# Moving the stream and one weight tile of the feed-forward products to other start addresses in SBUF

## The chip, the cores and the metric

The kernel runs on one core of one Trainium2 chip. The metric is the device time of one execution in microseconds, median of several runs. "Profiled execution" is one run taken with the hardware profiler; its span goes from the first to the last instruction.

## The reference

One decoder layer on 512 positions of 1024 channels: a gated short convolution and a sparse attention are merged into the residual stream, and then a convolutional feed-forward block follows. The change touches the feed-forward block alone, which is

```python
h = rmsnorm(x, norm2_g[l])
gu = h @ w_ffn_in[l]
g = causal_dwconv(gu[..., :D_FF], ffn_conv_w[l]) + ffn_conv_b[l]
x = x + (jax.nn.silu(g) * gu[..., D_FF:]) @ w_ffn_out[l]
```

with `D_FF` = 2816, that is 22 tiles of 128 channels, for the gate half and for the up half of `w_ffn_in`.

## The kernel before

**Precision.** Every operand of a large product is kept as two float32r tiles, a rounded one (`..h`) and the rest (`..l`). A product is three matmuls for each block of 128 input channels: high weight by high stream, high weight by low stream, low weight by high stream. `dense` (L402) issues the first two for all blocks (L405, L406), and then the third for all blocks (L408). In the profile the instructions carry these three lines, whatever product they belong to, so one goes by tile names.

**The products.** `h @ w_ffn_in` is made in blocks of 2 x 2 with seven products in place of eight (Strassen's scheme in Winograd's form). The stream is the normed input: `xf_h` and `xf_l` (L829, L830) hold for each of 4 blocks of input channels 7 forms of 256 positions, T4, B11 and so on, and they stay in SBUF for the whole stage. The weights come for two channel tiles `f`, `f+1` at a time. `ff_forms` (L898) loads two raw tiles and makes from them the seven weight forms: a22 as `th`/`tl` (two buffers, half the width), a11 and a12 side by side in the ring tiles `wh_s`/`wl_s`, and the four sums in `sh`/`sl`. `ff_pair` (L942) then runs the seven products, each with 4 blocks of input channels, so 12 matmuls of 256 moving columns against 128 x 128 weights, and adds the results on VectorE. Their PSUM banks are called `p1`, `p26`, `p45`, `p37`; the profile leaves numbers out and calls them all `p`. The first product of a pass is a22 by T4 (L977), on `th` and `tl`; then a11 and a12, on `wh_s` and `wl_s`; then the sums, on `sh` and `sl`.

**The order of the stage.** `ff_strassen` (L992) is called for f = 0, 2, ... 20. It makes a pass for the gate half (n = 0) and one for the up half (n = 1), so there are 22 passes of 84 matmuls. Behind each pass `between` runs at most one piece of the down projection by `w_ffn_out` (`down_part`, L1013), whose matmuls have 512 moving columns and write `pdn`. Pieces exist from f = 4 on; the scheduler that orders the instructions put some of the early ones in the middle of a pass. From f = 8 on each pass is followed by two tiles of the down projection, 24 matmuls of `pdn`, and then by the `th` matmuls of the next pass.

**Where things lie.** A tile pool lays its tiles out in SBUF one behind the other, in the order in which their tags first appear, so an unused tile of the right size moves all that follows in its pool. Such tiles are called `gap_..` here. Most tiles are multiples of 512 bytes a partition, and so it is enough to speak of a start as so many bytes behind a multiple of 512. Almost all matmul operands of this kernel begin at 480, the stationary ones and the moving ones, the down projection's included. In the program before, `gap_x` (80 words, 320 bytes) stands ahead of `xf_h` and `xf_l`, which so begin at bytes 37152 and 65824 of each partition, both 288 behind a multiple of 512. The pool `pw` follows. A placeholder named `th_` takes the two `th` buffers first, at 94496 and 96544, also 288 behind. Then `gap_w` (48 words, 192 bytes) brings all later tiles, `tl`, `sh`, `sl` and the rest, back to 480. `wh_s` and `wl_s` lie in another pool, at 480 too. Inside the tiles, the pieces that a matmul reads are 512 or 1024 bytes apart, so they begin at the same distance as their tile.

Of the kernel before, what the change touches and what calls it, by code (L numbers as in the profile page):

```python
# [11 lines left out]
F32 = mybir.dt.float32  # L12
# [6 lines left out]
P = 128  # L19
# [63 lines left out]
def tile_block(ctx: ExitStack, tc: tile.TileContext, xT, pos, par, par2, w_tok, w_a3, w_gate, w_ao, w_bo, w_o,  # L83
# [12 lines left out]
    def const(shape, name, dt=F32, pool=sb):  # L96
        return pool.tile(shape, dt, name=name, tag=name)
# [724 lines left out]
    B11, T4, B21, B22, T1, T3, T2 = range(7)  # L822
    px = ctx.enter_context(tc.tile_pool(name="px", bufs=1, side="left"))
    x1 = pxg.tile([P, KD, S], F32, name="x1", tag="xg_h", bufs=1)
    const([P, 80], "gap_x", F32, px)
    O_ORDER = (0, 4, 1, 5, 2, 6, 3, 7)
    for j in O_ORDER:
        nc.sync.dma_start(x1[:, j], xT[:, j])
    xf_h = const([P, 4, 7, TH], "xf_h", F32R, px)  # L829
    xf_l = const([P, 4, 7, TH], "xf_l", F32R, px)  # L830
    pw = ctx.enter_context(tc.tile_pool(name="pw", bufs=1, side="left"))
    pw.tile([P, D // 2], F32R, name="th_", tag="th", bufs=2)
    const([P, 48], "gap_w", F32, pw)

    def x_forms(k, v):
        nc.vector.tensor_sub(v[:, T1:T3 + 1], v[:, 1:4:2], v[:, 0:2])
# [273 lines left out]
```

## Time and profile before

| | us |
|---|---|
| median of 3 runs | 715.39 |
| lowest and highest | 714.96, 718.07 |
| profiled execution | 715.21 |
| its span | 713.5 |

The page counts 4285 matmuls (PE) and as many weight loads (PEld), 957 instructions on VectorE (DVE), 722 on ScalarE (ACT) and 179 on GpSimd (POOL). The feed-forward products run from about 363 to 682 us of the span. The timeline merges neighbouring equal instructions into a row with a count; a row's first number is the start of its first instruction in us. The length of a single matmul that the profile gives (276 to 284 ns for the feed-forward products) is longer than the distance to the next start, because matmuls are pipelined and their ends are modelled.

### The profile page before, as it was taken

How to read it: one execution, taken by the hardware profiler on the slowest of the kernel's cores; microseconds unless marked ns; L12 is line 12 of the kernel's file. 1: busy time of each engine (PE TensorE's matmuls, PEld its weight loads, DVE VectorE, ACT ScalarE, POOL GpSimd, SP SyncE). 2: the span in 40 equal slices, each digit the busy share in tenths (PEclk: the TensorE clock that was granted, in tenths of full speed). 3: DMA queues.
4: the chain of work that ended last, by engine and by line, in shares of the span. 5: the costliest groups of instructions: out<-in, count | busy, mean ns of one | idle time of the engine just before them, and what ended most of it. 6: DMA issues, size and time to landing. Idle time of an engine off the chain costs nothing.

```text
span 713.5 us, 11375 instructions
## 1 busy us (share of the span) xinstructions
PE 708.3 (99%) x4285; PEld 633.5 (89%) x4285; DVE 534.8 (75%) x957; ACT 432.6 (61%) x722; POOL 182.4 (26%) x179
## 2 busy tenths in 40 slices
PE   9999999999999999999999999999999999999997
PEld 9999878888888888888889999899999999999986
DVE  6887886687566878365795899988787877878643
ACT  7535655977667776522676767666555765647440
POOL 4051422133433334433012220221211222111110
PEclk9999999999999999999999999999999999999999
DMA  7333687511121122336386797987978779785565
GB/s 274 97 95 119 172 181 162 135 60 59 60 69 51 60 76 73 118 128 197 94 197 137 174 236 196 226 209 183 213 183 211 175 185 206 185 198 105 123 142 149
DMA packets 41142, 105.47 MB, mean 148 GB/s; under 512 B 3968, under 2 KB 9216, under 8 KB 41088
## 3 DMA queue, kind: packets, MB, share of 16 engines
q1 hardware_dynamic: 26528, 70.41, 30.4%
q0 software_dynamic: 14272, 34.08, 27.6%
q8 instruction: 33, 0.54, 0.3%
q10 hardware_dynamic: 288, 0.26, 0.1%
q14 instruction: 21, 0.17, 0.1%
HBM read 102.64 MB, written 2.10 MB: 147 GB/s over the span
## 4 chain that ended last, share of the span: by engine, by line
PE 96%; DMA 2%; ACT 1%; issue 0%; DVE 0%; POOL 0%; ACTq 0%; POOLq 0%
PE p L406 9%; PE p L405 9%; PE p L408 9%; PE pdn L406 6%; PE pdn L405 6%; PE pdn L408 6%; PE pg L406 4%; PE pg L405 4%; PE pg L408 4%; PE pa L405 2%; PE pt L681 2%; PE pa L406 2%; PE pa L408 2%; PE po L405 2%; PE po L406 2%; PE po L408 2%
## 5 line engine op out<-in xcount | busy, mean ns | idle before, releaser
L406 PE MATMUL p<-xf_l,sh 128*128 128x256 f32 x336 | 80.6, 277 | 0.0
L405 PE MATMUL p<-xf_h,sh 128*128 128x256 f32 x336 | 80.5, 277 | 0.0
L153 ACT ACTIVATE sh<-s 128x1024 fp32r<-128x1024 f32 x44 | 46.2, 1057 | 38.2 <-PE p L406 24.7
L406 PE MATMUL pdn<-al,wh_d 128*128 128x512 f32 x176 | 68.8, 391 | 0.0
L405 PE MATMUL pdn<-ah,wh_d 128*128 128x512 f32 x176 | 68.5, 390 | 0.0
L405 PEld LDWEIGHTS p<-xf_h,sh 128*128 128x128 f32 x336 | 63.0, 188 | 0.1
L406 PEld LDWEIGHTS p<-xf_l,sh 128*128 128x128 f32 x336 | 63.0, 188 | 0.1
L161 POOL DMA_DIRECT2D wl_s<-in_w_ff_dram x22 | 19.5, 885 | 167.2 <-ACT wl_s L160 155.9
L154 DVE TENSOR_TENSOR sl<-s,sh 128x1024 fp32r<-128x1024 f32 x44 | 53.8, 1224 | 8.7 <-ACT sh L153 8.7
L159 ACT ACTIVATE wh_s<-wr_s 128x1024 fp32r<-128x1024 f32 x22 | 23.3, 1059 | 53.1 <-PE pdn L406 50.1
L408 PE MATMUL p<-xf_h,sl 128*128 128x256 f32 x336 | 51.5, 277 | 0.0
L136 POOL TENSOR_TENSOR wl_g<-wr_g,wh_g 128x1024 fp32r<-128x1024 f32 x16 | 38.4, 2401 | 50.7 <-ACT wh_g L134 25.4
L405 PE MATMUL pg<-xg_h,wh_g 128*128 128x512 f32 x128 | 50.7, 396 | 0.0
L406 PE MATMUL pg<-xg_l,wh_g 128*128 128x512 f32 x128 | 50.6, 395 | 0.0
L408 PE MATMUL pdn<-ah,wl_d 128*128 128x512 f32 x176 | 47.7, 389 | 0.0
L161 POOL DMA_DIRECT2D wl_d<-in_w_dn_dram x22 | 26.5, 1203 | 77.2 <-ACT wl_d L160 69.0
L1029 DVE TENSOR_TENSOR x<-x,pdn 128x512 f32<-128x512 f32 x48 | 33.0, 688 | 16.2 <-PE pdn L408 15.5
L408 PEld LDWEIGHTS p<-xf_h,sl 128*128 128x128 f32 x336 | 44.6, 188 | 0.2
L405 PE MATMUL p<-xf_h,wh_s 128*128 128x256 f32 x168 | 40.5, 276 | 0.0
L406 PE MATMUL p<-xf_l,wh_s 128*128 128x256 f32 x168 | 40.5, 276 | 0.0
L408 PEld LDWEIGHTS pdn<-ah,wl_d 128*128 128x128 f32 x176 | 33.0, 188 | 6.9
L406 PEld LDWEIGHTS pdn<-al,wh_d 128*128 128x128 f32 x176 | 33.0, 188 | 6.2
(359 smaller groups left out, 2123.1 us busy)
## 6 DMA issues: line engine op xcount, KB each, us to landing
wr_s<-in_w_ff_dram SPq DMA_DIRECT2D x44, 512.0 KB, 4.9
wl_s<-in_w_ff_dram POOLq DMA_DIRECT2D x22, 512.0 KB, 7.2
wr_d<-in_w_dn_dram SPq DMA_DIRECT2D x22, 512.0 KB, 7.0
wl_d<-in_w_dn_dram POOLq DMA_DIRECT2D x22, 512.0 KB, 8.2
wr_g<-in_w_gate_dram SPq DMA_DIRECT2D x16, 512.0 KB, 3.4
wr_a<-in_w_a_dram SPq DMA_DIRECT2D x12, 512.0 KB, 4.1
tl<-in_w_ff_dram POOLq DMA_DIRECT2D x22, 256.0 KB, 6.9
wl_a<-in_w_a_dram POOLq DMA_DIRECT2D x10, 512.0 KB, 7.9
```

The source lines that it names most:

```text
L136: e.tensor_sub(lo[:, 0:n], raw[:, 0:n], hi[:, 0:n].bitcast(F32))
L153: hi = nc.scalar.activation(h, v, AF.Copy)
L154: nc.vector.tensor_sub(l, v, h.bitcast(F32))
L159: nc.scalar.activation(h, raw, AF.Copy)
L161: nc.gpsimd.dma_start(l if dst is None else dst, src, accum_op=ALU.add)
L405: nc.tensor.matmul(acc, wh, xh, start=first and i == 0, stop=False)
L406: nc.tensor.matmul(acc, wh, xl, start=False, stop=False)
L408: nc.tensor.matmul(acc, wl, xh, start=False, stop=last and i == len(units) - 1)
L681: nc.tensor.transpose(pt[:, i * P:(i + 1) * P], e[:, i, (kt + k0) * P:(kt + k0 + 1) * P], ident)
L1029: nc.vector.tensor_add(xj, xj, acc)
```

## The change

Two unused tiles change size, and one of them changes place. `gap_x` becomes 112 words, 448 bytes, so `xf_h` and `xf_l` begin at 37280 and 65952, 416 behind a multiple of 512. `gap_w` becomes 16 words, 64 bytes, and stands ahead of `th_`, so the two `th` buffers begin at 94688 and 96736, 480 behind. The two gaps together are 128 words before and after, so no other tile moves. The instructions of every engine and their order are the same in both programs.

```diff
@@ -822,15 +822,15 @@
     px = ctx.enter_context(tc.tile_pool(name="px", bufs=1, side="left"))
     x1 = pxg.tile([P, KD, S], F32, name="x1", tag="xg_h", bufs=1)
-    const([P, 80], "gap_x", F32, px)
+    const([P, 112], "gap_x", F32, px)
     O_ORDER = (0, 4, 1, 5, 2, 6, 3, 7)
...
     pw = ctx.enter_context(tc.tile_pool(name="pw", bufs=1, side="left"))
+    const([P, 16], "gap_w", F32, pw)
     pw.tile([P, D // 2], F32R, name="th_", tag="th", bufs=2)
-    const([P, 48], "gap_w", F32, pw)
```

## The prediction

> **What bounds the kernel now.** I read the page's first two parts and the chain that ended last, then the windows of the feed-forward stage, then the timeline of TensorE row by row.
>
> ```profile
> PE 708.3 (99%) x4285; PEld 633.5 (89%) x4285; DVE 534.8 (75%) x957; ACT 432.6 (61%) x722; POOL 182.4 (26%) x179
> PEclk9999999999999999999999999999999999999999
> PE 96%; DMA 2%; ACT 1%; issue 0%; DVE 0%; POOL 0%; ACTq 0%; POOLq 0%
> ```
>
> TensorE works without a break, at full clock, and is 96% of the chain. So only the pace at which one matmul follows another can move the end; the other engines, the queues and the DMAs do the same work as before and have room. The busy time of a matmul is modelled and says little here. What counts is the distance from one start to the next, which I call the pitch.
>
> The edit moves the two moving tiles of the products `p` (`xf_h`, `xf_l`) and one weight tile (`th`). How many of these matmuls stand where is shown by the windows of the instructions that write `p` (columns: stretch, length, busy time and count of matmuls, clock, DMA):
>
> ```profile
> 359.50:397.50 38.00, 21.02 (x170) 1.00 0.75 163
> 397.50:420.50 23.00, 23.00 (x204) 1.00 0.80 194
> 420.50:437.50 17.00, 15.34 (x130) 1.00 0.89 225
> 437.50:477.50 40.00, 21.51 (x175) 1.00 0.90 214
> 477.50:683.50 206.00, 136.15 (x1176) 1.00 0.78 180
> ```
>
> By the code there are 22 passes (11 values of `f`, times gate and up) of 84 matmuls, 1848 in all, each with 256 moving columns: 12 on `th`/`tl`, and 72 on the other forms. The windows add to 1855 because a matmul across an edge counts twice.
>
> **Three paces of the same matmul.** The timeline of one pass late in the stage (start, length of the merged row, line, operation, count; a row of x4 is four matmuls):
>
> ```profile
> 476.65 1.07 PE L408 MATMUL pdn<-ah,wl_d 128*128 128x512 f32 x4
> 477.55 0.28 PE L405 MATMUL p<-xf_h,th 128*128 128x256 f32 x1
> 477.67 0.28 PE L406 MATMUL p<-xf_l,th 128*128 128x256 f32 x1
> ...
> 478.50 0.62 PE L408 MATMUL p<-xf_h,tl 128*128 128x256 f32 x4
> 478.96 0.28 PE L405 MATMUL p<-xf_h,wh_s 128*128 128x256 f32 x1
> ...
> 487.12 0.39 PE L405 MATMUL pdn<-ah,wh_d 128*128 128x512 f32 x1
> ```
>
> Eight matmuls with `th` take 477.55 to 478.50, 0.95/8 = 118.8 ns each. The 72 that follow take 478.96 to 487.12, 8.16/72 = 113.3 ns. The `pdn` matmuls ahead have 512 columns and take (477.55 - 476.65)/4 = 225 ns, the same per column: this is the stream's own pace, and nothing I found in the feed-forward stage goes below it for long. Call 113.3 the fast pace.
>
> An earlier pass, whose last `th` matmul alone stands behind a down projection:
>
> ```profile
> 462.11 1.07 PE L408 MATMUL pdn<-ah,wl_d 128*128 128x512 f32 x4
> 463.02 0.28 PE L406 MATMUL p<-xf_l,th 128*128 128x256 f32 x1
> 463.14 0.63 PE L408 MATMUL p<-xf_h,tl 128*128 128x256 f32 x4
> 463.61 0.28 PE L405 MATMUL p<-xf_h,wh_s 128*128 128x256 f32 x1
> ...
> 472.09 0.39 PE L405 MATMUL pdn<-ah,wh_d 128*128 128x512 f32 x1
> ```
>
> The same 72 matmuls, on the same tiles at the same addresses, take 463.61 to 472.09: 8.48/72 = 117.8 ns. TensorE waits for nobody in either pass. So there are two stable paces for one and the same pair of addresses (moving at 288 behind a multiple of 512, weights at 480), and a pass stays in the one it fell into for its whole length. What decides is how it was entered. Behind eight `th` matmuls, whose weights also lie at 288, it runs fast. Where a down projection hands over straight to a weight at 480, it runs slow. Two more such hand-overs:
>
> ```profile
> 421.71 0.28 PE L405 MATMUL p<-xf_h,sh 128*128 128x256 f32 x1
> ...
> 426.19 0.40 PE L406 MATMUL p<-xf_l,sh 128*128 128x256 f32 x2
> ...
> 450.65 0.28 PE L406 MATMUL p<-xf_l,sh 128*128 128x256 f32 x1
> 450.77 0.28 PE L405 MATMUL p<-xf_h,sh 128*128 128x256 f32 x1
> 450.88 0.28 PE L406 MATMUL p<-xf_l,sh 128*128 128x256 f32 x1
> 451.00 0.28 PE L408 MATMUL p<-xf_h,sl 128*128 128x256 f32 x1
> 451.12 0.39 PE L405 MATMUL pdn<-ah,wh_d 128*128 128x512 f32 x1
> ```
>
> The four at 450.65 take 0.47 us, 117.5 ns each; the stretch from 421.71 to 426.19, 38 matmuls, (426.19 - 421.71)/38 = 117.9 ns. I found no hand-over from a settled down projection to a weight at 480 that ran fast at once.
>
> When `th` follows a fast pass directly it is slower still, 406.84 to 407.80, 0.96/8 = 120 ns, and yet the 72 behind it run fast (408.26 to 416.42, 8.16 us):
>
> ```profile
> 406.84 0.28 PE L405 MATMUL p<-xf_h,th 128*128 128x256 f32 x1
> ...
> 407.80 0.62 PE L408 MATMUL p<-xf_h,tl 128*128 128x256 f32 x4
> 408.26 0.28 PE L405 MATMUL p<-xf_h,wh_s 128*128 128x256 f32 x1
> ...
> 416.42 0.28 PE L405 MATMUL p<-xf_h,th 128*128 128x256 f32 x1
> ```
>
> So `th` at the address of the moving operand costs 118.8 - 113.3 = 5.5 ns a matmul, and at the same time sets the rest of the pass on the fast pace. My reading, which is an inference: the weight load of the next matmul and the moving stream of this one get in each other's way, by how their addresses and starts stand to each other, and the slow pace is the one in which the weight load is late.
>
> **The change part by part.** No instruction is added, removed or reordered on any engine, and no DMA; only three kinds of address differ.
>
> (a) `th` goes from 288 to 480. What it removes is the price of equal addresses: 22 passes x 8 x 5.5 ns = 0.97 us, if these matmuls then run at the fast pace. What goes with it is the cover: the kick that put 14 of 14 passes behind 477.5 on the fast pace. After the change each such pass is a hand-over from a down projection straight to a weight at 480, the kind that ran slow in each case above.
>
> (b) `xf_h` and `xf_l` go from 288 to 416, so that the weights at 480 begin 64 bytes ahead of the stream instead of 192. The trace has no such pair for a 256-column product. From above it is bounded by the dearest pace seen, 120 ns; from below by the stream's own, 113.3. The nearest rows are the two paces of the pair 288 and 480, since there too stream and weights begin apart; between them I take the slow one, because of (a), and keep both ends. That other distances act alike is suggested by the scores, where 512 columns start at 352 in one place and at 96 in another, both against weights at 480 and both entered from settled projections:
>
> ```profile
> 99.45 0.40 PE L602 MATMUL sc<-kk,qT 128*128 128x512 f32 x1
> 99.69 0.39 PE L603 MATMUL sc<-kk,qT 128*128 128x512 f32 x1
> 99.91 0.40 PE L602 MATMUL sc<-kk,qT 128*128 128x512 f32 x1
> ...
> 127.14 0.40 PE L602 MATMUL sc<-kk,qT 128*128 128x512 f32 x1
> 127.37 0.39 PE L603 MATMUL sc<-kk,qT 128*128 128x512 f32 x1
> 127.59 0.39 PE L405 MATMUL pa<-xg_h,wh_a 128*128 128x512 f32 x1
> ```
>
> The two matmuls take 0.46 us at 352 and 0.45 us at 96: at these two distances the address makes no difference.
>
> **The sum for the likeliest case**, all passes slow. Behind 477.5: 1176 matmuls, 14 x 8 = 112 of them on `th`. 1064 x (117.8 - 113.3) ns = +4.8 us, 112 x (117.8 - 118.8) = -0.1 us. Between 397.5 and 437.5: 334 matmuls less about 38 that are slow already and 32 on `th`: 264 x 4.5 = +1.2 us. Before 397.5 and from 437.5 to 477.5 the passes are slow already: nothing. Together +5.9 us; small differences in how the down projections settle I put at -0.2 us (an estimate). The profiled execution took 715.21 us (713.5 us of span and 1.7 around it), close to the median of 715.39. 715.2 + 5.7 = 720.9 us. The ACT, DVE and POOL work beside it gets 0.3 us more time a pass, so nothing new waits.
>
> **The rivals.**
>
> *All passes fast* (faster side). If 64 bytes apart settles on 113.3 ns from any entry, `th` gains 0.97 us and the slow stretches go: 170 + 175 + 38 matmuls less about 45 on `th`, 338 x 4.5 ns = 1.5 us. 715.2 - 2.5 = 712.7 us. For it: the fast pace exists for weights at 480, and all weights now stand alike to the stream. Against it: the hand-overs above. It decides at the first `tl` of a pass behind a down projection.
>
> *A part of each pass slow*: a pass enters slow and settles after some products. Half of them would give half of 5.9 less 0.4 for `th`: about 717.7 us. Against it: the 8.48 us above shows no settling in 72 matmuls.
>
> *Addresses do nothing at this distance*, so that what is won on `th` and lost on the kick cancel: 715.3 us.
> The Trainium skill, "TensorE: Matmul & The Clock Gate", Part 2 (What happens when you issue a matmul), says that TensorE has two independent read ports, and that loading the next weights takes no read bandwidth from the running matmul; by that rule no address in this edit matters and the time stays at 715.2. The trace does not agree: the same 256 columns run at 113.3 and at 118.8 ns, and what differs between the two sets of weights is their start address.
>
> *Too near*: 64 bytes act like no distance, and every matmul takes the 120 ns that `th` takes behind a fast pass. From 113.3 that is 6.7 ns x (1064 + 264) = 8.9 us, from 117.8 2.2 x 338 = 0.7, and `th` 0.2: 725.0 us. For it: of the distances possible this one is next to zero. Against it: the stream leaves the start within a few ns.
>
> *Better than the fast pace*: some wait still lies inside the 113.3 ns. No row of these products shows it, so I can price only its edge: below 711.8 us.
>
> **How the numbers follow.** All slow 0.40 (719.5 to 721.8), a part slow 0.09, all fast 0.32, nothing 0.06, too near 0.07, better 0.06. A measurement of this kernel tells about 0.5%, 3.6 us, from no change. Slower by more than that: all slow and too near, 0.47. Faster by more: better, and a tail of 0.03 of all fast, 0.09. Within: the rest, 0.44. The cases have both signs, so the range goes from all fast to all slow, 712.0 to 721.8, and leaves out about 0.16.
>
> **What would show it.** In the profile after: the eight `th` matmuls should lose their own pace and run like their neighbours (right in every case but "too near"). The stretch from the first `wh_s` to the next `pdn` should take 8.5 us in a pass behind 477.5; 8.2 us there means the fast pace, and the forecast falls; 8.6 us or more means "too near". Counts, DMA and the other engines' busy time should stay. What would make me wrong is a settling that depends on the stream's start as well as on the entry, which no row here can show.

## The result and the profile after

| | before | after |
|---|---|---|
| median of 6 runs each (us) | 715.4 | 720.0 |
| lowest, highest (us) | 714.84, 718.07 | 718.95, 723.28 |
| profiled execution (us) | 715.21 | 721.54 |
| its span (us) | 713.5 | 719.7 |

The changed kernel is slower: ratio 1.0071, 95% interval 1.0057 to 1.0084. The forecast was 720.9 us in a range of 712.0 to 721.8. The times compared in this text are of runs at a granted clock of 0.997 or more; one at a lower clock, the profiled execution of `lead_2` below at 0.851, is left out.

Two lines of the page of after, busy time by engine and the chain that ended last:

```profile
PE 712.6 (99%) x4285; PEld 638.1 (89%) x4285; DVE 535.0 (74%) x957; ACT 432.8 (60%) x722; POOL 183.1 (25%) x179
PE 96%; DMA 2%; POOL 1%; ACT 1%; SPq 0%; DVE 0%; issue 0%; ACTq 0%
```

Counts are equal, the other engines are as busy as before, and TensorE is still 96% of the chain. Busy time of TensorE grew by 4.3 us, the span by 6.2. So not all of the growth is matmuls that follow each other more slowly. Four marks in the timelines tell where it came from: the first feed-forward matmul, the first `pdn`, a later `pdn`, and the `pdn` behind the last pass. Before:

```profile
363.91 0.28 PE L969 MATMUL p<-xf_h,sh 128*128 128x256 f32 x1
...
420.55 0.39 PE L405 MATMUL pdn<-ah,wh_d 128*128 128x512 f32 x1
...
436.67 0.39 PE L405 MATMUL pdn<-ah,wh_d 128*128 128x512 f32 x1
...
682.46 0.39 PE L405 MATMUL pdn<-ah,wh_d 128*128 128x512 f32 x1
```

The same instructions after, and ahead of them a row with a wait (in brackets: idle time in us, and what ended it):

```profile
81.81 0.50 PE L408 MATMUL pa<-xg_h,wl_a 128*128 128x512 f32 x1 [1.89 <-DMA wl_a<-in_w_a_dram]
...
365.85 0.28 PE L969 MATMUL p<-xf_h,sh 128*128 128x256 f32 x1
...
422.21 0.39 PE L405 MATMUL pdn<-ah,wh_d 128*128 128x512 f32 x1
...
438.62 0.39 PE L405 MATMUL pdn<-ah,wh_d 128*128 128x512 f32 x1
...
688.70 0.39 PE L405 MATMUL pdn<-ah,wh_d 128*128 128x512 f32 x1
```

The stage begins 1.94 us later (365.85 - 363.91), because the DMA of a weight tile landed late in a product long ahead of it. It ends 6.24 us later. So the stage itself is longer by 4.30 us: 322.85 us in place of 318.55. Up to the first `pdn` it gains (56.36 in place of 56.64), up to the mark at 436.67 before (438.62 after) it has lost that again (72.77 in place of 72.76), and the whole growth, 250.08 - 245.79 = 4.29 us, lies behind. The early wait lies outside the stage, and the runs of after, 718.95 to 723.28 us, spread by more than it. In kernels below with the same stream and `th` addresses the stage begins at 363.85 and 364.38, so these addresses alone do not bring it about.

A pass behind 477.5 in the timeline of after, the one whose rows before began at 477.55:

```profile
476.76 0.39 PE L405 MATMUL pdn<-ah,wh_d 128*128 128x512 f32 x1
...
479.48 0.28 PE L405 MATMUL p<-xf_h,th 128*128 128x256 f32 x1
...
480.42 0.64 PE L408 MATMUL p<-xf_h,tl 128*128 128x256 f32 x4
480.89 0.28 PE L405 MATMUL p<-xf_h,wh_s 128*128 128x256 f32 x1
...
489.37 0.39 PE L405 MATMUL pdn<-ah,wh_d 128*128 128x512 f32 x1
```

The eight on `th` take 0.94/8 = 117.5 ns each, and the 72 behind take 489.37 - 480.89 = 8.48 us, 117.8 ns, against 8.16 us before. All 14 passes behind 477.5 run so. The twelve `pdn` ahead take 2.72/12 = 226.7 ns.

An earlier stretch of after:

```profile
412.74 0.28 PE L405 MATMUL p<-xf_h,sh 128*128 128x256 f32 x1
...
413.19 0.70 PE L408 MATMUL p<-xf_h,sl 128*128 128x256 f32 x4
413.73 0.28 PE L405 MATMUL p<-xf_h,sh 128*128 128x256 f32 x1
...
415.97 0.28 PE L406 MATMUL p<-xf_l,sh 128*128 128x256 f32 x1
```

Up to 413.19 the pitch is (413.19 - 412.74)/4 = 113 ns; it had been so from about 383, in products that before the change ran at 117.8 ns until about 397.5. The four from 413.19 take 0.54 us, about 0.09 more than at that pace, and behind them it is (415.97 - 413.73)/19 = 117.9 ns, with the same tiles at the same addresses. So the pair 416 and 480 knows both paces too. Here the change of pace goes with one start that comes late, but that a late start is the cause is not shown: in the kernel `mv_160` below the five matmuls from 410.65 to 411.39 also take 0.17 us more than at the fast pace, and the twelve behind them run at (412.75 - 411.39)/12 = 113.3 ns again.

### The profile page after: what moved, and what is told of

Same layout as the page of the kernel before. It is cut to its first block, busy times and chain, and to the rows that moved or that the text cites. A ratio compares the mean times of both kernels' runs of the same rounds, so it can differ in the third digit from the quotient of the medians.

```text
span 719.7 us, 11375 instructions
## 1 busy us (share of the span) xinstructions
PE 712.6 (99%) x4285; PEld 638.1 (89%) x4285; DVE 535.0 (74%) x957; ACT 432.8 (60%) x722; POOL 183.1 (25%) x179
## 4 chain that ended last, share of the span: by engine, by line
PE 96%; DMA 2%; POOL 1%; ACT 1%; SPq 0%; DVE 0%; issue 0%; ACTq 0%
PE p L405 10%; PE p L408 10%; PE p L406 10%; PE pdn L406 6%; PE pdn L405 6%; PE pdn L408 6%; PE pg L406 4%; PE pg L405 4%; PE pg L408 4%; PE pa L408 3%; PE pa L405 3%; PE pa L406 3%; PE pt L681 2%; PE po L405 2%; PE po L406 2%; PE po L408 2%
## 5 line engine op out<-in xcount | busy, mean ns | idle before, releaser
L406 PE MATMUL p<-xf_l,sh 128*128 128x256 f32 x336 | 82.5, 281 | 0.0
L405 PE MATMUL p<-xf_h,sh 128*128 128x256 f32 x336 | 82.4, 281 | 0.0
```

The source lines that it names most:

```text
L405: nc.tensor.matmul(acc, wh, xh, start=first and i == 0, stop=False)
L406: nc.tensor.matmul(acc, wh, xl, start=False, stop=False)
```

## The experiments

All were timed in three rounds beside the kernel before. Each pace is read from one profiled execution of its kernel. "Stage" is the time in the trace from the first feed-forward matmul to the `pdn` behind the last pass (before: 318.55 us); it leaves out what happened ahead of it. The 14 passes behind 477.5 are called the late ones; "72" is the time from the first `wh_s` to the next `pdn` in one of them. Starts are given as bytes behind a multiple of 512, and the distance is from the stream to the weights of the 72.

| | stream, `th` | time (us) | ratio, interval | stage | 72 (us) |
|---|---|---|---|---|---|
| before | 288, 288 | 715.4 | 1 | 318.55 | 8.16 |
| after | 416, 480 | 720.0 | 1.0071 (1.0057 to 1.0084) | 322.85 | 8.48 |
| th_only | 288, 480 | 721.24 | 1.007 (1.0053 to 1.0087) | 324.38 | 8.48 |
| equal_416 | 416, 416 | 720.66 | 1.0066 (1.0051 to 1.0081) | 323.66 | 8.48 |
| th_288 | 416, 288 | 715.0 | 0.9991 (0.9982 to 1.0001) | 317.75 | 8.16 |
| all_480 | 480, 480 | 724.84 | 1.0122 (1.0106 to 1.0137) | 328.22 | 8.64 |
| mv_352 | 352, 480 | 725.13 | 1.0137 (1.012 to 1.0153) | 327.96 | 8.64 |
| mv_160 | 160, 480 | 719.55 | 1.0061 (1.0046 to 1.0076) | 322.64 | 8.48 |
| lead_2 | 416, 480 | 722.61 | 1.0103 (1.0086 to 1.012) | | |
| lead_128 | 416, 480 | 722.4 | 1.01 (1.0085 to 1.0115) | 325.72 | 8.48 |
| dn_416_after | 416, 480 | 716.81 | 1.0019 (1.001 to 1.0029) | 318.95 | 8.16 |
| dn_416_before | 288, 288 | 717.9 | 1.0036 (1.0022 to 1.0049) | 320.37 | 8.16 |
| dn_352_after | 416, 480 | 716.8 | 1.0021 (1.0011 to 1.0031) | 318.94 | 8.16 |
| dn_224_after | 416, 480 | 719.42 | 1.0052 (1.0037 to 1.0067) | 322.46 | 8.48 |

### Part (a) alone: `th` to 480, the stream stays

```diff
-    const([P, 112], "gap_x", F32, px)
+    const([P, 80], "gap_x", F32, px)
...
-    const([P, 16], "gap_w", F32, pw)
+    const([P, 48], "gap_w", F32, pw)
     pw.tile([P, D // 2], F32R, name="th_", tag="th", bufs=2)
```

(The diff is against the changed kernel, as are those that follow.)

> The stream stays at 288, the th weights go to 480 (first half of the change alone). Theory (the pace of a pass is set at its entry, and eight th matmuls at the stream's own address are what set it on the fast pace): every pass behind a down projection runs at 117.8 ns, 8.48 us for the 72 matmuls, as in the changed kernel; 719 to 721 us. Rival (the new address of the stream makes the slow pace): the passes run at 113.3 ns, th included, 713 to 715 us.

The timeline of the pass behind 477.5:

```profile
483.52 0.28 PE L405 MATMUL p<-xf_h,wh_s 128*128 128x256 f32 x1
...
492.00 0.40 PE L405 MATMUL pdn<-ah,wh_d 128*128 128x512 f32 x1
```

8.48 us: with the old stream address, all 14 passes behind 477.5 are slow once `th` has left 288. This one part does the whole damage. The stream at 416 even softens it, by 324.38 - 322.85 = 1.5 us of the stage, 1.1 of them ahead of the later `pdn` mark (73.83 us up to there, in place of 72.77).

### Is it the equal address? `th` and stream both at 416

```diff
-    const([P, 16], "gap_w", F32, pw)
     pw.tile([P, D // 2], F32R, name="th_", tag="th", bufs=2)
+    const([P, 16], "gap_v", F32, pw)
```

> The stream goes to 416 and th with it, so that th and stream begin at equal distances again; the other weights stay at 480. Theory (it counts that th and stream are equal): th at 118 to 120 ns, the 72 matmuls behind it at 113.3 ns, 8.16 us; 714.5 to 716 us. Rival (it counts that th is at 288, or the stream): slow passes, 719 to 721 us.

```profile
479.95 0.28 PE L405 MATMUL p<-xf_h,th 128*128 128x256 f32 x1
...
480.90 0.64 PE L408 MATMUL p<-xf_h,tl 128*128 128x256 f32 x4
481.37 0.28 PE L405 MATMUL p<-xf_h,wh_s 128*128 128x256 f32 x1
...
489.85 0.39 PE L405 MATMUL pdn<-ah,wh_d 128*128 128x512 f32 x1
```

`th` pays its price again (0.95/8 = 118.8 ns), and yet the 72 take 8.48 us, as in all 14 passes behind 477.5. So eight matmuls at the stream's own address do not set the fast pace by themselves. My reading on record falls here.

The pass ahead of these, which has a single matmul on `th` behind the down projection, is fast all the same in this kernel:

```profile
465.74 0.28 PE L406 MATMUL p<-xf_l,th 128*128 128x256 f32 x1
...
466.33 0.28 PE L405 MATMUL p<-xf_h,wh_s 128*128 128x256 f32 x1
...
474.50 0.39 PE L405 MATMUL pdn<-ah,wh_d 128*128 128x512 f32 x1
```

Its 72 take 474.50 - 466.33 = 8.17 us. So one kernel has both paces for the same pair of addresses, and what differs is how the pass was entered.

### `th` back at 288, the stream at 416

```diff
-    const([P, 16], "gap_w", F32, pw)
+    const([P, 96], "gap_w", F32, pw)
     pw.tile([P, D // 2], F32R, name="th_", tag="th", bufs=2)
+    const([P, 48], "gap_v", F32, pw)
```

> The stream goes to 416, th stays at 288 (second half of the change alone; the pool grows by 512 bytes a partition). Theory (th apart from the stream sets nothing): passes at 117.8 ns, th too, 719 to 721 us. Rival (th at 288 is what helps, wherever the stream is): the 72 matmuls at 113.3 ns, 714.5 to 716 us.

```profile
477.74 0.28 PE L405 MATMUL p<-xf_h,th 128*128 128x256 f32 x1
...
479.15 0.28 PE L405 MATMUL p<-xf_h,wh_s 128*128 128x256 f32 x1
...
487.31 0.39 PE L405 MATMUL pdn<-ah,wh_d 128*128 128x512 f32 x1
```

8.16 us. The 72 matmuls are those of the changed kernel, on the same tiles at the same distance (the tiles behind `th` lie 512 bytes further), and differ in one thing: eight matmuls on another weight address ran ahead of them. So the entry, what ran just ahead, decides the pace. It also gives back the loss: 715.0 us, the same as before within the interval.

### No distance at all, and other distances

```diff
-    const([P, 112], "gap_x", F32, px)
...
-    const([P, 16], "gap_w", F32, pw)
```

> No gap at all: stream and every weight form at 480. Theory (equal addresses cost what th cost before): 118 to 120 ns for all 84 matmuls of a pass, so no fast pace is left; 720 to 725 us. Rival (equal addresses are harmless as such): 113.3 ns and 712 to 714 us.

```profile
481.44 0.28 PE L405 MATMUL p<-xf_h,wh_s 128*128 128x256 f32 x1
...
490.08 0.40 PE L405 MATMUL pdn<-ah,wh_d 128*128 128x512 f32 x1
```

8.64/72 = 120.0 ns, the third pace, now for all products: equal addresses cost 6.7 ns a matmul against the fast pace. Next, two distances of which no row before told anything, 128 bytes (`gap_x` 96 words, `gap_w` 32) and 320 bytes (48 and 80):

> Stream at 352, every weight form at 480 (128 bytes ahead of the stream). Theory (every distance but zero has both paces, and an entry straight from a settled down projection gives the slow one): 117.8 ns, 719 to 721.5 us. Rival (the distance decides, and some are always fast): 113.3 ns, 712 to 714 us.

> Stream at 160, every weight form at 480 (320 bytes ahead of the stream, the farthest from 416 on this side). Theory: slow, 719 to 721.5 us. Rival: fast, 712 to 714 us.

At 128 bytes:

```profile
481.67 0.28 PE L405 MATMUL p<-xf_h,wh_s 128*128 128x256 f32 x1
...
490.31 0.39 PE L405 MATMUL pdn<-ah,wh_d 128*128 128x512 f32 x1
```

8.64 us, 120.0 ns, here as an alternation of starts 117, 120 and 123 ns apart. Theory and rival were both wrong here: behind 477.5 a distance of 128 bytes costs what none does. Earlier in the stage it does not quite: from 390 to 422 us the same pair runs at 118.7 ns, where all_480 already has 120.0. At 320 bytes the theory held: the kernel behaves like the changed one, fast early passes included, and the stage takes 322.64 us against 322.85. So of the distances tried 0 and 128 give 120 ns in the late passes, and 64, 192 and 320, the odd multiples of 64, give the pair of 113.3 and 117.8.

### A lead matmul behind the down projection

If the point in time of the first start decides, one short matmul more at the head of a pass might shift it. I added one of 2, and in another kernel of 128 columns, on `th`, at the head of 21 passes; its result is overwritten by the product that follows.

```diff
+        if late is None:
+            nc.tensor.matmul(b45[:, 0:128], form["a22"][0][:, 0:P], xf_h[:, 0, T4, 0:128], start=True, stop=True)
         product(b45[:, lo], "a22", T4)
```

> The changed kernel with one matmul of 2 moving columns more at the head of each pass but the first (21 in all, on the first th block, into a bank that the pass opens anew); no address moves. Each should cost about what a weight load allows, 112 ns, 2.4 us in all. Theory (a pass keeps the pace that its entry gives it): another entry can give the fast pace at the same addresses; then the 72 matmuls behind it take 8.16 us and the kernel 716 to 717.5 us; if this entry too falls outside the fast pace's reach, 722 to 723 us. Rival (stream at 416 and weights at 480 fix the pace): 8.48 us a pass, 722 to 723 us with every entry.

> The same with 128 columns in the leading matmul, so that the pass starts at another moment after the down projection. Theory: as for 2 columns, and fast or slow by itself; at least one of the two fast, 716 to 717.5 us. Rival: slow, 722 to 723.5 us.

With 128 columns (the lead is the row with L978):

```profile
478.53 0.22 PE L978 MATMUL p<-xf_h,th 128*128 128x128 f32 x1
478.59 0.33 PE L405 MATMUL p<-xf_h,th 128*128 128x256 f32 x1
478.76 0.28 PE L406 MATMUL p<-xf_l,th 128*128 128x256 f32 x1
...
480.05 0.28 PE L405 MATMUL p<-xf_h,wh_s 128*128 128x256 f32 x1
...
488.53 0.40 PE L405 MATMUL pdn<-ah,wh_d 128*128 128x512 f32 x1
```

Lead and first matmul together take 0.23 us in place of 0.118, so the lead costs 0.112 us, 21 of them 2.4, and 720.0 + 2.4 = 722.4 is what was measured. The pass behind it is as slow as without. The 2-column lead cost the same by its time, and no pitch is read from it. So my expectation that at least one of the two would make the late passes fast, and the kernel 716 to 717.5 us, was wrong: behind the down projection the lead of 128 columns reached no fast entry.

Earlier in the same trace, where a pass follows the pass before directly, the pace does change at the leads. Ahead of the first one shown here it was slow ((396.42 - 395.83)/5 = 118 ns):

```profile
395.83 0.28 PE L406 MATMUL p<-xf_l,sh 128*128 128x256 f32 x1
...
396.42 0.22 PE L978 MATMUL p<-xf_h,th 128*128 128x128 f32 x1
...
398.83 0.28 PE L405 MATMUL p<-xf_h,wh_s 128*128 128x256 f32 x1
...
406.99 0.22 PE L978 MATMUL p<-xf_h,th 128*128 128x128 f32 x1
...
408.51 0.28 PE L405 MATMUL p<-xf_h,wh_s 128*128 128x256 f32 x1
...
416.99 0.22 PE L978 MATMUL p<-xf_h,th 128*128 128x128 f32 x1
```

The 72 behind the first of these leads take 406.99 - 398.83 = 8.16 us, and the 72 behind the second take 416.99 - 408.51 = 8.48 us, in one kernel at the same addresses. Without a lead, in the timeline of after, the pace stays fast over that stretch, until 413.19. (With a lead the scheduler also placed some early pieces of the down projection elsewhere.)

### Another down projection ahead of the same passes

A cleaner way to change the entry is to touch only what runs ahead. Here the down projection's stream `ah`, `al` goes from 480 to 416, and the feed-forward products keep every address.

```diff
+    const([P, 112], "gap_a", F32, pf)
     a_tiles(0)
+    const([P, 16], "gap_b", F32, pf)
```

> The changed kernel (stream 416, weights 480) with the down projection's stream moved from 480 to 416, its weights left at 480, by two unused tiles of 448 and 64 bytes. Theory (how a down projection settles sets the entry of the pass behind it, at unchanged addresses of that pass): the start of the th matmuls against the settled pdn matmuls changes, and passes behind 477.5 us may run at 113.3 ns, 8.16 us for the 72; 714 to 716 us then, else 720. Rival (pace fixed by the pass's own addresses): 8.48 us, 720 us. Aside: if a distance of 64 bytes also lets 512 columns run at less than 226.7 ns, by up to the 6.7 ns that equal addresses cost 256 columns, 527 x 6.7 = 3.5 us come off in any case.

```profile
476.72 0.28 PE L405 MATMUL p<-xf_h,th 128*128 128x256 f32 x1
...
478.08 0.28 PE L405 MATMUL p<-xf_h,wh_s 128*128 128x256 f32 x1
...
486.24 0.39 PE L405 MATMUL pdn<-ah,wh_d 128*128 128x512 f32 x1
...
489.04 0.39 PE L405 MATMUL pdn<-ah,wh_d 128*128 128x512 f32 x1
```

The 72 take 8.16 us, and no pass behind 477.5 is slow any more, `th` included ((478.08 - 476.72)/12 = 113 ns), at the very addresses at which all were slow after the change. The other expectation, that the down projection itself would gain at 64 bytes, was wrong: its 12 matmuls take 2.80 us, 233.3 ns, in place of 226.7. By that, 528 matmuls (176 for each of its three lines) would lose 528 x 6.6 ns = 3.5 us. By the starts in the two traces, the passes of the stage gain 6.3 us and the `pdn` lose 2.4 us in it and 0.8 us behind it, about half of the gain, and 716.8 us stay.

The same edit in the kernel before (`gap_x` 80 words, `th_` ahead of a `gap_w` of 48):

> The kernel before (stream and th 288, other weights 480) with the down projection's stream at 416 in the same way. Theory: the eight th matmuls start from another settled state, so the passes behind 477.5 us may leave the fast pace (8.48 us, 720 us) or stay on it (715 us). Rival (th at 288 sets the fast pace whatever is ahead): 8.16 us, 715 us. Aside as for the other: 3.5 us less if 512 columns gain from the distance.

```profile
478.84 0.28 PE L405 MATMUL p<-xf_h,wh_s 128*128 128x256 f32 x1
...
487.00 0.39 PE L405 MATMUL pdn<-ah,wh_d 128*128 128x512 f32 x1
```

There `th` at 288 still sets the fast pace behind this other down projection (8.16 us), and the price of `pdn` alone remains: 717.9 us.

Last, two distances at which the down projection might hand over well without losing pace itself, 128 bytes (`gap_a` 96 words, `gap_b` 32) and 256 bytes (64 and 64):

> The changed kernel with the down projection's stream (ah, al) moved from 480 to 352 behind a multiple of 512, that is 128 bytes from its weights at 480; the feed-forward passes keep their addresses. No work is changed. What the earlier runs leave open is whether the down projection can hand over at another point of the start grid without losing pace itself. Theory (512 columns lose pace at odd multiples of 64 bytes only, and where a settled down projection ends decides the pace of the pass behind it): the pdn matmuls keep 226.7 ns, and if 128 bytes shift the point at which they settle, the passes behind go fast (72 matmuls in 8.16 us): 720.0 - 1176 x 4.5 ns = about 714.5 us. Rival 1 (128 bytes act like none for 512 columns): pdn at 226.7 ns and at the same point, passes slow (8.48 us): 720 us, as the changed kernel. Rival 2 (for 512 columns any distance costs): pdn at 230 ns or more, +2 to +3.4 us: about 717 us with fast passes, 722 us with slow ones.

> The same with ah and al at 224, that is 256 bytes from their weights. Theory: pdn at 226.7 ns; passes either fast, about 714.5 us, or slow, 720 us, by the point at which the down projection settles. If 128 and 256 bytes give the same pace of pdn and the same pace of the passes, only the remainder by 128 counts for 512 columns; if they differ, the theory that goes by the remainder alone falls. Rival 2: pdn at 230 ns or more, 717 us or 722 us.

At 128 bytes:

```profile
477.13 0.28 PE L405 MATMUL p<-xf_h,th 128*128 128x256 f32 x1
...
478.49 0.28 PE L405 MATMUL p<-xf_h,wh_s 128*128 128x256 f32 x1
...
486.65 0.40 PE L405 MATMUL pdn<-ah,wh_d 128*128 128x512 f32 x1
...
489.45 0.40 PE L405 MATMUL pdn<-ah,wh_d 128*128 128x512 f32 x1
```

At 256 bytes:

```profile
479.02 0.28 PE L405 MATMUL p<-xf_h,wh_s 128*128 128x256 f32 x1
...
487.50 0.39 PE L405 MATMUL pdn<-ah,wh_d 128*128 128x512 f32 x1
...
490.22 0.39 PE L405 MATMUL pdn<-ah,wh_d 128*128 128x512 f32 x1
```

128 bytes: fast passes, slow down projection (2.80/12 = 233.3 ns). That is rival 2 of the expectation, and its theory was wrong. 256 bytes: slow passes (8.48 us), and `pdn` at 2.72/12 = 226.7 ns. So the remainder by 128 bytes, which sorted the distances of the 256-column products, does not sort those of the 512-column ones. In the four kernels with the stream at 416, `th` at 480 and no lead, the late passes are fast where the down projection ahead runs at 233 ns, and slow where it runs at 226.7. No layout tried has both fast; a version clearly better than the kernel before was not found.

## Why the prediction was right

**TensorE's pitch alone decides.** Right: counts, chain and the other engines stayed, and the stage grew by what its matmuls grew.

**(a) `th` loses its own price and with it the kick.** Right, and shown from both sides. Taking `th` away from 288 alone makes every late pass slow (th_only), and putting it back alone makes every late pass fast (th_288). That two paces exist for the same pair of addresses and that the entry chooses is shown by dn_416_after, where only `ah` and `al` moved, and by th_288 and the leads in lead_128. What was wrong is the name I gave to the kick, `th` at the stream's own address: at 416 for both all 14 late passes are slow, at 288 against 416, which are 128 bytes apart, all are fast. What must run ahead for a fast entry stays open. So does my inference that in the slow pace the weight load is late: in the trace of before the weight loads have a mean length of 188 ns in the slow pass from 463.61 and in the fast one from 478.96 alike, and no run took this apart.

**(b) The stream at 64 bytes takes the slow pace of its nearest rows.** Right behind 477.5, wrong from 383 to 413.2, and the support I called was weak. The two score pairs, 0.46 and 0.45 us, are too short to show a difference of a few ns. mv_352 shows that distance does matter (120.0 ns at 128 bytes), and the down projection shows it for 512 columns (233.3 against 226.7). The rival "too near" had its price right, 725.0 us, but at 0 and 128 bytes (724.84 and 725.13 us), not at 64. The rival "all passes fast" was nearer than it looked: these passes do run fast behind another down projection. It needed the entry to differ, which the edit didn't bring about behind 477.5.

**The sum.** Behind the mark at 436.67 I had +4.8 - 0.1 - 0.2 = +4.5 us, and measured was +4.29. By the starts in the two traces, 1064 x (117.78 - 113.33) ns = 4.73, `th` 112 x (117.7 - 118.6) = -0.10, and the down projections -0.34, where I had put -0.2 as an estimate. A slow pass hands over to a `pdn` that has its 226.7 ns at once, while behind a fast pass of the kernel before the first starts of `pdn` are 231, 236, 228 and 233 ns apart, and the mean is 227.7.

**The step that failed** is the early part: "Between 397.5 and 437.5 ... +1.2 us. Before 397.5 and from 437.5 to 477.5 the passes are slow already: nothing." Measured from the first feed-forward matmul to the mark at 436.67: 0.01 us in all. I took for granted that the early passes would be slow for the new pair as well. They went onto the fast pace at about 383 and stayed there till 413.2, which gained in stretches that had been slow, and then lost as much.

So the mechanism is worth 4.3 us in the traces, and 715.2 + 4.3 = 719.5 us; 720.9 was too high by that early term. Between the medians lie 4.6 us, by the ratio 5.1. The rest can be the waits ahead of the stage, of which the profiled execution had 1.9 us; how much of them the other runs had is not recorded, and stays open. That 720.0 lies only 0.9 us from 720.9 is thus in part luck: the early term that failed was made up for in part by time that the sum did not have.

**The rule on the ports.** The prediction set the Trainium skill's two independent read ports (TensorE: Matmul & The Clock Gate, Part 2: What happens when you issue a matmul) against a trace in which addresses mattered. The runs bear the trace out: the same instructions in the same order, with only start addresses changed, took 715.0, 720.0 and 724.84 us. The Trainium skill, SBUF — State Buffer, in the section Door 1: The DMA port swizzle (why `[64,N]` ≈ `[32,N]`), says that SBUF is read in lines of 16 bytes. Every start here is a multiple of 32 bytes, so by that all would be alike, while the runs tell 64 from 128 bytes.

## What to carry to other kernels

Where matmuls follow each other without a break, read the distances between their starts: modelled durations hide a loss of 4% that the address of an operand, or merely what ran just ahead, can cause. Before a small irregularity is tidied away (here one tile at an odd address that by the estimate cost 1 us), remove it alone: it may be what sets the pace of its neighbours. And judge a layout by all products that share the engine, because a gain in one (fast passes behind a shifted down projection) was taken back by the other.

## What the runs showed of the hardware

- A matmul of 256 columns follows the one before after 113.3, 117.8 or 120.0 ns in the late passes. Stream and weights 0 or 128 bytes apart (modulo 512) settle on 120.0 there (128 bytes on 118.7 in the early part), at 64, 192 or 320 on one of the other two. Which of the two is set at the entry and held through all 14 late passes of every kernel with these distances whose paces were read; in one case shown, at 413.19 in the timeline of after, it changed within a stretch.
- A matmul of 512 columns has 226.7 ns at 0 and 256 bytes, and starts 231 and 236 (64 bytes) or 237 and 229 ns (128 bytes) apart in turn, 233.3 on the mean.
- The settled pitches are whole multiples of 6.67 ns: 17 (113.3), 18 (120.0), 34 (226.7) and 35 (233.3); the slow pace is 53 for three matmuls (117.8). This is arithmetic on the measured pitches, and no run tells what the step is.
